# Start of a two-layer trunk kernel: all tokens loaded and transposed first, a one-block first conditioning, and two leading tiles per weight place

## The chip, the cores and the metric

The kernel runs on one core of a Trainium2 chip. The metric is the device time of one execution in microseconds (us). The engines that matter here are TensorE (PE, matrix products; it loads its stationary operand with separate instructions, PEld), VectorE (DVE), ScalarE (ACT), GpSimd (POOL) and SyncE (SP), which issues most of the DMA transfers. Each engine takes its own queue in order.

## The reference

A diffusion trunk of two layers over 128 prompt tokens and 512 sample tokens, 2048 wide. Each layer is

```python
m = silu(cond) @ ada_w[layer] + ada_b[layer]      # shift, scale, gate: 3 x 2048, one for c_ctx, one for c
h = rms_norm(x, norm_g[layer]) * (1.0 + scale) + shift
x = x + gate * (mixer(h @ w_in) @ w_out)
```

with `rms_norm` over the 2048 features of a token. Layer 0's `w_in` has 2048 rows and 6656 columns. The columns feed banded attention with a sink (query, key, value, gate) and a gated short convolution (u, b, c and a gate); layer 1 has a differential attention and a dense one. All is float32. The outputs are the new tokens and the prompt's keys and values.

Only the very start of layer 0 is touched by the change: making `h` of the 640 tokens, and the first products with `w_in`.

## The kernel before

**Layout.** Products are taken with features on the partitions: `h` is needed as 16 feature blocks (k = 0 to 15) of 128 partitions by 640 tokens, so the tokens, which lie in memory row by row, are first transposed on PE, 128 by 128 at a time. A float32 product is made of three products with split operands (`hi*hi`, `lo*hi`, `hi*lo`, lines 263 to 265): a weight tile is split on ACT (`wh`, line 227) and DVE (`wl`, line 228), and so is `h` (lines 1009 and 1010). The 640 tokens go through in two halves of 320, one for each PSUM bank (`pa`, `pb`; in the first unit the tile is called `pf`).

**Conditioning.** Shift and scale of a feature block are themselves products, of the conditioning vectors with columns of `ada_w`. `ada_on_pe` (line 173) multiplies all 16 row blocks of some columns (line 180), copies the result (line 183), transposes it back (line 186), and makes `mod` and `gsc` from it (lines 163 and 151). The loads go through four buffers of 1 MB (`ada_t`).

**Leading tiles.** While the conditioning still comes in, the kernel cannot run one output tile through all 16 feature blocks. It runs eight output tiles ("leads") side by side instead: eight *units* of two feature blocks each, and in each unit all eight leads. Two leads (`held`) keep their PSUM banks throughout. Six (`TRANS`) share the banks `pa`, `pb`: after each unit their result is added to a sum in SBUF (line 399; in the first unit it is copied, line 355). The order of the eight is sum, held, sum, held, sum, sum, sum, sum. After the first lead of a unit stands the conditioning of the next unit (`ahead`, that is `ada_group`, two column groups of 256 columns).

**Start.** Before the first unit, `first_loads` (line 975) issues the loads of scale and shift for feature blocks 0 and 1 and the first weights, transposes token blocks 0 to 2 (`x_block`, line 939: transposes at line 946, copies to `xT` at 947, sums of squares at 951), and spreads the normalisation factors over the partitions with rank-one products (`x_rows`, line 959). Token blocks 3 and 4 are loaded behind that; their transposes and squares (line 936) are put between the leads of the first unit by `between` (line 991). `first_unit` (line 331) runs the first unit by halves: tokens 0 to 319 of both feature blocks through all leads, then tokens 320 to 639.

**Weight places.** A place is a buffer of the ring `raw`, `wh`, `wl` with four each (`W_BUFS = 4`), 512 elements per partition. In the first unit a place holds two leads (`first_raws`, 2 leads x 2 blocks x 128 columns); in units 1 to 7 it holds one lead (`load_raw`, 2 blocks x 128), so half of it is unused.

**Order.** The order in which an engine takes its instructions comes from a list scheduler: the program order gives the priority, and an instruction that could start earlier is put ahead. `tc.issue_after` keeps some instructions behind a given one. Buffers are handed out by the same scheduler.

Of the kernel before, what the change touches and what calls it, by code (L numbers as in the profile page):

```python
# [20 lines left out]
P = 128  # L21
D = 2048
KT = D // P
NS = 512
# [26 lines left out]
def trunk_kernel(ctx: ExitStack, tc: tile.TileContext, I: dict, O: dict):  # L51
# [57 lines left out]
    xs = [x_load(b) for b in range(3)]  # L109
# [36 lines left out]
    def ada_done(l, cb, h=0, n=4):  # L146
        fs = slice(cb * 4 + 2 * h, cb * 4 + 2 * h + n)
        which, k0 = cb // 4, (cb % 4) * 4 + 2 * h
# [12 lines left out]
    def add_bias(l, cb, red, h=0, n=4):  # L161
        fs = slice(cb * 4 + 2 * h, cb * 4 + 2 * h + n)
        V.tensor_tensor(mod[l][:, fs, :], red, ada_b[l][:, fs][:, :, None].to_broadcast([P, n, 2]), op=ALU.add)
# [9 lines left out]
    def ada_on_pe(l, cb, h=0, n=4, ws=None):  # L173

        acc, m, wd = psT(), 16 // n, n * P
        for kt in range(KT):
            if kt % m == 0:
                w = ws[kt // m] if ws else ada_load(l, cb, kt, h, n)
# [11 lines left out]
        add_bias(l, cb, red, h, n)  # L190
        ada_done(l, cb, h, n)

    def ada_on_dve(blocks):

        for l, cb in blocks:
# [12 lines left out]
            for b in range(2):  # L208
# [11 lines left out]
                for h in range(2):  # L220
                    add_bias(l, cb + b, t[:, h, :, :, 0], h, 2)
# [103 lines left out]
    def first_raws(w_ap, cols, js):  # L325
        raw = wpool.tile([P, 2, 2, P], F32, tag="raw", name="raw")
        for i, col in enumerate(cols):
            nc.sync.dma_start(raw[:, i], w_ap[js[0] * P:js[1] * P, col:col + P].rearrange("(k p) n -> p k n", p=P))
        return raw

    def first_unit(raws, leads, trans, pps, make_h, ahead, units, between):

        pos, qd, js = units[0]
        parts = {}

        def split_two(i):
            with tc.issue_after(last_act[0].ins):
                wh, wl = split_w(raws[i])
            for j in range(2):
                parts[leads[2 * i + j]] = wh[:, j], wl[:, j]  # L340

        split_two(0)
        split_two(1)
        for half_i, sl in HV:
            for k in range(*js):
                make_h(k, half_i)
            for i, n in enumerate(leads):
                if not half_i and i in (0, 2):
                    split_two(2 + i // 2)
                if half_i and n == leads[1]:  # L350
                    ahead(*units[1][1:])
                if n in trans:
                    pp = {half_i: pproj.tile([P, 512], F32, tag="p%s0" % "ab"[i % 2], name="pf")}
                    proj_q(pp, parts[n], qd, pos, [(half_i, sl)], alone=True, js=js)
                    last_act[0] = A.copy(pps[n][half_i], pp[half_i][:, 0:HALF])
# [5 lines left out]
    def run_tiles(jobs, w_ap, make_h, fill=None, rate=0.0, ahead=None, order=(0, 1, 2, 3), before=None,  # L361
                  last=None, by_half=False, mid=False, trans=[], grace=0, cut=None, summed=None, led=None, freed=None,
                  n_lead=3, first=None, between=None):
# [13 lines left out]
        units = [(pos, qd, js) for pos, qd in enumerate(order) for js in (cut or [(0, 4)])] if leads else []  # L377
        for ui, (pos, qd, js) in enumerate(units):
            if first and ui == 0:
                first_unit(first, leads, trans, pps, make_h, ahead, units, between)  # L380
                continue
            raws = {n: load_raw(w_ap, jobs[n][0], qd, js) for n in leads[:W_BUFS]}
            parts = {n: split_w(raws[n]) for n in raws}
            for hv in [HV[:1], HV[1:]] if by_half and pos == 0 else [HV]:
                for k in range(4 * qd + js[0], 4 * qd + js[1]):
                    make_h(k, hv) if by_half else make_h(k)
                for n in leads:
                    if ahead and n == leads[1] and ui + 1 < len(units):
# [1406 lines left out]
```

## Time and profile before

| | |
|---|---|
| time, median of 3 runs | 2289.66 us (2288.84 to 2295.46) |
| profiled execution, its own time | 2289.15 us |
| its span, first to last instruction | 2287.4 us |
| PE busy | 2251.7 us, 98% |
| DVE, ACT, POOL busy | 70%, 48%, 7% |
| DMA, mean over the span | 150 GB/s; 308 GB/s in the first 70 us |

A line of a timeline gives start, length, engine, line of the kernel, operation, written tile <- read tiles, shapes and count, and in brackets how long the engine had been idle before and what ended that. A line of a group gives count, busy time, the mean of one in ns, and the idle time before. Products on PE overlap: the length of one is longer than the distance to the next.

### The profile page before, as it was taken

Reading aid. Unit: us, or ns where it says so; the run is one execution under the profiler, and the core shown is the slowest. Engines: PE = TensorE matmul, PEld = TensorE weight load, DVE = VectorE, ACT = ScalarE, POOL = GpSimd, SP = SyncE. Lnnn points to the kernel's source line nnn. Section 1 sums busy time; section 2 is a strip of 40 time slices with the busy share of each in tenths; the row PEclk is TensorE's granted clock in tenths of the full one; section 3 lists DMA queues with packets and bytes.
Section 4 is the critical chain, followed back from the end, with each engine's and each line's share of the span. In section 5 each row is a group of like instructions: output and inputs, shape, how many; then the busy total and the mean of one; then the engine's idle time right before and its main releaser. Section 6 shows DMA issues by size and latency. Waiting matters only on the chain.

```text
span 2287.4 us, 41077 instructions
## 1 busy us (share of the span) xinstructions
PE 2251.7 (98%) x15877; PEld 2175.1 (95%) x15877; DVE 1600.2 (70%) x2845; ACT 1093.0 (48%) x2317; POOL 162.3 (7%) x226
## 2 busy tenths in 40 slices
PE   7999999999999999999999999999999999999999
PEld 5889999999999999999999999999999999999999
DVE  4666969779779777787797666565666655557765
ACT  5225535244352222544474444465565676755443
POOL 1001000010000000000100001111111100000101
PEclk9999999999999999999999999999999999999999
DMA  9875545655537564865553334423223221238642
GB/s 336 265 243 195 175 151 167 184 157 170 178 118 238 178 187 144 265 179 147 170 150 114 115 113 115 142 67 100 83 64 97 71 62 51 74 103 268 182 137 62
DMA packets 381300, 344.21 MB, mean 150 GB/s; under 512 B 16418, under 2 KB 338432, under 8 KB 380592
## 3 DMA queue, kind: packets, MB, share of 16 engines
q1 hardware_dynamic: 366528, 296.66, 43.2%
q0 software_dynamic: 13856, 42.76, 5.4%
q8 instruction: 125, 2.05, 0.4%
q10 hardware_dynamic: 720, 2.16, 0.3%
q14 instruction: 71, 0.58, 0.1%
HBM read 301.93 MB, written 39.59 MB: 149 GB/s over the span
## 4 chain that ended last, share of the span: by engine, by line
PE 47%; ACT 3%; issue 2%; DVE 2%; DMA 2%; POOL 0%; SPq 0%; POOLq 0%; DVEq 0%; ACTq 0%
PE pq L585 7%; PE pq L584 7%; PE pq L583 7%; PE pb L278 2%; PE pb L277 2%; PE pa L277 2%; PE pb L279 2%; PE pa L279 2%; PE pa L278 2%; PE T L787 1%; PE T L612 1%; PE S L799 1%; PE S L801 1%; PE S L800 1%; PE pa L264 1%
## 5 line engine op out<-in xcount | busy, mean ns | idle before, releaser
L227 ACT ACTIVATE wh<-raw 128x512 fp32r<-128x512 f32 (+1 forms) x446 | 268.8, 603 | 554.7 <-PE pb L264 386.0
L228 DVE TENSOR_TENSOR wl<-raw,wh 128x512 fp32r<-128x512 f32 (+1 forms) x446 | 291.4, 654 | 208.8 <-ACT wh L227 185.8
L263 PE MATMUL pa<-h,wh 128*128 128x320 f32 x980 | 311.0, 318 | 3.6 <-ACT h L227 2.0
L264 PE MATMUL pa<-h,wh 128*128 128x320 f32 x980 | 306.1, 313 | 3.1 <-DVE h L228 2.1
L265 PE MATMUL pa<-h,wl 128*128 128x320 f32 x980 | 304.4, 311 | 0.0
L264 PE MATMUL pb<-h,wh 128*128 128x320 f32 x980 | 303.1, 309 | 0.0
L265 PE MATMUL pb<-h,wl 128*128 128x320 f32 x980 | 303.0, 309 | 0.0
L263 PE MATMUL pb<-h,wh 128*128 128x320 f32 x980 | 302.9, 310 | 0.0
L205 DVE SCALAR_TENSOR_TENSOR acc<-adaw,sT,acc 128x1024 f32<-128x1024 f32 x240 | 299.9, 1276 | 0.0
L583 PE MATMUL pq<-h,wh 128*128 128x320 f32 x672 | 208.7, 311 | 0.4 <-ACT wh L227 0.4
L585 PE MATMUL pq<-h,wl 128*128 128x320 f32 x672 | 207.9, 309 | 0.2 <-DVE wl L228 0.2
L584 PE MATMUL pq<-h,wh 128*128 128x320 f32 x672 | 207.6, 309 | 0.0
L263 PEld LDWEIGHTS pa<-h,wh 128*128 128x128 f32 x980 | 184.6, 189 | 16.5 <-issue 10.4
L264 PEld LDWEIGHTS pa<-h,wh 128*128 128x128 f32 x980 | 185.0, 189 | 10.0 <-DVE h L228 4.1
L263 PEld LDWEIGHTS pb<-h,wh 128*128 128x128 f32 x980 | 183.8, 188 | 1.8 <-issue 1.2
L265 PEld LDWEIGHTS pa<-h,wl 128*128 128x128 f32 x980 | 184.8, 189 | 0.4 <-issue 0.4
L264 PEld LDWEIGHTS pb<-h,wh 128*128 128x128 f32 x980 | 183.9, 188 | 0.2
L265 PEld LDWEIGHTS pb<-h,wl 128*128 128x128 f32 x980 | 184.0, 188 | 0.0
L585 PE MATMUL pq<-T,wl 128*128 128x320 f32 x504 | 155.1, 308 | 0.2 <-DVE wl L228 0.2
L584 PE MATMUL pq<-T,wh 128*128 128x320 f32 x504 | 155.3, 308 | 0.0
L583 PE MATMUL pq<-T,wh 128*128 128x320 f32 x504 | 155.0, 308 | 0.1
L277 PE MATMUL pa<-h,wh 128*128 128x320 f32 x448 | 146.1, 326 | 0.0
(452 smaller groups left out, 5399.9 us busy)
## 6 DMA issues: line engine op xcount, KB each, us to landing
adaw<-in_ada_w SPq DMA_DIRECT2D x128, 512.0 KB, 4.2
raw<-in_ev_w_in SPq DMA_DIRECT2D x176, 256.0 KB, 3.5
raw<-in_od_w_in SPq DMA_DIRECT2D x154, 256.0 KB, 2.9
ada<-in_ada_w SPq DMA_DIRECT2D x32, 1024.0 KB, 7.6
w<-in_od_w_in SPq DMA_DIRECT2D x27, 512.0 KB, 3.9
yd<-y POOLq DMA_DIRECT2D x32, 320.0 KB, 3.4
yin<-yd SPq DMA_DIRECT2D x32, 320.0 KB, 4.3
w<-yd SPq DMA_DIRECT2D x32, 320.0 KB, 3.9
```

The source lines that it names most:

```text
L205: V.scalar_tensor_tensor(out=acc[c], in0=w, scalar=sT[:, kt, c:c + 1], in1=acc[c], op0=ALU.mult, op1=ALU.add)
L227: A.activation(hi, x, AF.Copy)
L228: V.tensor_sub(lo, x, hi)
L263: PE.matmul(ps, wh[:, i, :], hi[:, sl], start=(j == js[0] if alone else (pos == 0 and j == 0)), stop=False)
L264: PE.matmul(ps, wh[:, i, :], lo[:, sl], start=False, stop=False)
L265: last_mm[0] = PE.matmul(ps, wl[:, i, :], hi[:, sl], start=False, stop=(j == js[1] - 1 if alone else (pos == 3 and j == 3)))
L277: PE.matmul(ps, wh[:, j, :], hi[:, sl], start=(qd == 0 and j == 0), stop=False)
L278: PE.matmul(ps, wh[:, j, :], lo[:, sl], start=False, stop=False)
L279: PE.matmul(ps, wl[:, j, :], hi[:, sl], start=False, stop=(qd == 3 and j == 3))
L583: PE.matmul(ps, wh[:, j, :], hi, start=(new and h == 0 and j == 0), stop=False, **kw)
L584: PE.matmul(ps, wh[:, j, :], lo, start=False, stop=False, **kw)
L585: PE.matmul(ps, wl[:, j, :], hi, start=False, stop=(h == 1 and j == 3), **kw)
```

## The change

All five token blocks are loaded at the very start, ahead of conditioning and weights, and `first_loads` transposes all five before the first unit; `between` and the separate squares of blocks 3 and 4 are gone. Conditioning is addressed by feature block (`b0`) instead of by halves of four. The first conditioning covers feature block 0 alone (128 columns of scale, 128 of shift, one load of 1 MB each); that of block 1 stands after the first lead of the first unit. The first unit is run block by block, over all 640 tokens: block 0 through all leads, with results of the summed leads copied, then block 1 with results added. In all eight units a weight place holds two leads. The weights of the next unit are loaded during a unit, at leads 2, 3, 5 and 6, and the splits are made up to two places ahead.

```diff
-    xs = [x_load(b) for b in range(3)]
+    xs = [x_load(b) for b in range(5)]
...
-    def ada_load(l, cb, kt, h, n):
+    def ada_load(l, cb, kt, b0, n):
         m = 16 // n
         w = ada_t[0].rearrange("p (k n) -> p k n", k=m)
         ada_t.append(ada_t.pop(0))
-        nc.sync.dma_start(w, I["ada_w"][l, kt * P:(kt + m) * P, cb * 512 + h * 256:cb * 512 + h * 256 + n * P]
+        nc.sync.dma_start(w, I["ada_w"][l, kt * P:(kt + m) * P, cb * 512 + b0 * P:cb * 512 + (b0 + n) * P]
                           .rearrange("(k p) n -> p k n", p=P))
...
-    def first_unit(raws, leads, trans, pps, make_h, ahead, units, between):
...
-        split_two(0)
-        split_two(1)
-        for half_i, sl in HV:
-            for k in range(*js):
-                make_h(k, half_i)
-            for i, n in enumerate(leads):
-                if not half_i and i in (0, 2):
-                    split_two(2 + i // 2)
-                if half_i and n == leads[1]:
-                    ahead(*units[1][1:])
-                if n in trans:
-                    pp = {half_i: pproj.tile([P, 512], F32, tag="p%s0" % "ab"[i % 2], name="pf")}
-                    proj_q(pp, parts[n], qd, pos, [(half_i, sl)], alone=True, js=js)
-                    last_act[0] = A.copy(pps[n][half_i], pp[half_i][:, 0:HALF])
-                else:
-                    proj_q(pps[n], parts[n], qd, pos, [(half_i, sl)], js=js)
-                if not half_i:
-                    between(i)
+    def lead_units(raws, w_ap, jobs, leads, sums, pps, make_h, ahead, units, summed):
+
+        two = len(leads) // 2
+        cols = [(jobs[leads[2 * p]][0], jobs[leads[2 * p + 1]][0]) for p in range(two)]
+        parts = []
+
+        def split_to(q):
+            while len(parts) < 2 * min(q + 1, two * len(units)):
+                p = len(parts) // 2
+                with tc.issue_after(last_act[0].ins) if p < two else ExitStack():
+                    wh, wl = split_w(raws[p])
+                parts.extend((wh[:, j], wl[:, j]) for j in range(2))
+
+        def one_block(u, k, n, part, pp):
+            alone = n in sums
+            wh, wl = part
+            hi, lo = hs[k]
+            j = k % 2
+            for h, sl in HV:
+                ps = pp[h][:, 0:HALF]
+                PE.matmul(ps, wh[:, j, :], hi[:, sl], start=(alone or k == 0), stop=False)
+                PE.matmul(ps, wh[:, j, :], lo[:, sl], start=False, stop=False)
+                last_mm[0] = PE.matmul(ps, wl[:, j, :], hi[:, sl], start=False, stop=alone)
+
+        for ui, (pos, qd, js) in enumerate(units):
+            k0 = 4 * qd + js[0]
+            split_to(ui * two)
+            for c in range(2 if ui == 0 else 1):
+                ks = [c] if ui == 0 else [k0, k0 + 1]
+                for k in ks:
+                    make_h(k)
+                for i, n in enumerate(leads):
+                    if i == 1 and ui == 0 and c == 0:
+                        ahead(0, (1, 2))
+                    elif i == 1 and ui + 1 < len(units):
+                        ahead(*units[ui + 1][1:])
+                    if ui or not c:
+                        split_to(ui * two + min(i // 2 + 1, two - (ui == 0)))
+                    elif i == len(leads) - 2:
+                        split_to(two)
+                    if (ui or c) and i in (2, 3, 5, 6) and ui + 1 < len(units):
+                        _, q, j = units[ui + 1]
+                        raws.append(load_two(w_ap, cols[(2, 3, 5, 6).index(i)], 4 * q + j[0]))
+                    part = parts[2 * ui * two + i]
+                    pp = new_pp(0) if n in sums else pps[n]
+                    if ui == 0:
+                        one_block(ui, c, n, part, pp)
+                    else:
+                        proj_q(pp, part, qd, pos, alone=n in sums, js=js)
+                    if n in sums:
+                        for h, sl in HV:
+                            if ui == 0 and c == 0:
+                                last_act[0] = A.copy(sums[n][:, sl], pp[h][:, 0:HALF])
+                            else:
+                                V.tensor_add(sums[n][:, sl], sums[n][:, sl], pp[h][:, 0:HALF])
+                        summed(ui, n, pps[n])
...
     def first_loads(cols):
 
-        scale = [ada_load(0, 4, kt, 0, 2) for kt in (0, 8)]
-        raws = [first_raws(I["ev_w_in"][0], cols[i:i + 2], (0, 2)) for i in (0, 2)]
-        shift = [ada_load(0, 0, kt, 0, 2) for kt in (0, 8)]
-        raws += [first_raws(I["ev_w_in"][0], cols[i:i + 2], (0, 2)) for i in (4, 6)]
-        xs.extend(x_load(b) for b in (3, 4))
+        scale = [ada_load(0, 4, 0, 0, 1)]
+        raws = [load_two(I["ev_w_in"][0], cols[0:2], 0)]
+        shift = [ada_load(0, 0, 0, 0, 1)]
+        raws += [load_two(I["ev_w_in"][0], cols[i:i + 2], 0) for i in (2, 4, 6)]
         x_block(0, xs[0])
         vec_rows(0, 80, rows_a, 32)
-        x_block(1, xs[1])
-        x_block(2, xs[2])
-        ada_on_pe(0, 4, 0, 2, scale)
-        x_rows((0, 1, 2))
-        ada_on_pe(0, 0, 0, 2, shift)
+        for b in range(1, 5):
+            x_block(b, xs[b])
+        last_act[0] = put[0]
+        ada_on_pe(0, 4, 0, 1, scale)
+        x_rows((0, 1, 2, 3))
+        x_rows((4,))
+        vec_rows(80, 77, rows_b, 0)
+        ada_on_pe(0, 0, 0, 1, shift)
         return raws
```

More of the change, by code (lines that the diff above doesn't have):

```diff
@@ L377, in run_tiles @@
         units = [(pos, qd, js) for pos, qd in enumerate(order) for js in (cut or [(0, 4)])] if leads else []
+        if first:
+            lead_units(first, w_ap, jobs, leads, sums, pps, make_h, ahead, units, summed)
+            units = []
         for ui, (pos, qd, js) in enumerate(units):
[L379 to L382, printed above, removed]
+            raws = {n: load_raw(w_ap, jobs[n][0], qd, js) for n in leads}
             parts = {n: split_w(raws[n]) for n in raws}
@@ L1149, in trunk_kernel @@
     run_tiles(jobs, I["ev_w_in"][0], h0_maker, fill0, FILL0, ada_group, trans=TRANS, grace=GRACE, cut=((0, 2), (2, 4)),
-              summed=keep, led=even_start, freed=ada_start, first=raws, between=between)
+              summed=keep, led=even_start, freed=ada_start, first=raws)
     drain(prep)
```

94 lines of the change are left out of this document (27 added, 67 removed).

## The prediction

> **What bounds the kernel now.** I read the page first, then the busy time by stage, then the start of the kernel in order of time on TensorE (PE), VectorE (DVE) and ScalarE (ACT). The page, whose span is 2287.4 us:
>
> ```profile
> PE 2251.7 (98%) x15877; PEld 2175.1 (95%) x15877; DVE 1600.2 (70%) x2845; ACT 1093.0 (48%) x2317; POOL 162.3 (7%) x226
> ...
> PE   7999999999999999999999999999999999999999
> ```
>
> PE is busy for 98% of the span, and of the 40 slices only the first lacks its 9. I cut the span there: up to the first weight product (30.05), the first unit of the eight leading tiles (to 56.70), units 1 to 7 (to 187.60), and the rest, which the change does not touch:
>
> ```profile
> 0.00:30.05 30.05, 16.01 (x124) 9.90 (x124) 11.22 (x30) 12.73 (x24) 6.06 (x15) 0.94 0.98 337
> 30.05:56.70 26.65, 26.22 (x201) 21.86 (x202) 15.38 (x38) 17.66 (x46) 1.10 (x2) 0.94 1.03 336
> 56.70:187.60 130.90, 129.40 (x1082) 112.40 (x1080) 88.12 (x222) 38.69 (x94) 1.24 (x3) 1.00 0.78 249
> 187.60:2287.40 2099.80, 2080.10 (x14473) 2030.97 (x14472) 1485.46 (x2555) 1023.91 (x2155) 153.88 (x207) 1.00 0.46 139
> ```
>
> Columns: PE, weight loads, DVE, ACT, POOL, clock, DMA share, GB/s. The lead-in is bound by DMA (share 0.98, 337 GB/s, PE busy 16 of 30 us). From 30 us on PE is the bound. So the change is worth what it takes off PE after 30 us, plus what it does to the instant of the first product; what it moves into the lead-in is free as long as DMA still ends last there.
>
> The end of the lead-in:
>
> ```profile
> 25.99 1.82 PE L180 MATMUL T<-ada,sT 128*32 128x256 f32 x16 [1.78 <-DMA ada<-in_ada_w]
> 28.34 0.69 PE L186 MATMUL T<-ident,ada_sb 128*128 128x128 f32 x2 [0.53 <-ACT ada_sb L183]
> 30.09 0.64 PE L263 MATMUL pf<-h,wh 128*128 128x320 f32 x1 [1.06 <-ACT h L1009]
> ...
> 32.92 0.35 PE L263 MATMUL pa<-h,wh 128*128 128x320 f32 x1
> ```
>
> The second half of the shift weights lands at 25.99; products, two transposes and h follow, 4.1 us in all, and then the first product. The first 11 products take 2.83 us.
>
> **The lead-in, part by part.** What must land before the first product, by these issue rows:
>
> ```profile
> ada<-in_ada_w SPq DMA_DIRECT2D x13, 1024.0 KB, 9.1
> raw<-in_ev_w_in SPq DMA_DIRECT2D x20, 128.0 KB, 5.8
> xb<-in_x_sample ACTq DMA_DIRECT2D x4, 512.0 KB, 6.5
> ```
>
> Before: three token blocks (6 x 512 KB), four conditioning loads (4 x 1024 KB) and two weight places (4 x 128 KB), 7.9 MB. After: five token blocks (10 x 512 KB), two conditioning loads, one weight place, 7.6 MB. SP now issues blocks 3 and 4 ahead of all this, and the second weight place no longer stands ahead of the shift load; POOL's queue only gets two powers earlier. The 0.26 MB less are 0.75 us at 348 GB/s. Against it, the one-block conditioning is read in runs of 512 bytes where the two-block one has runs of 1024. DMA at work on the long runs, and in a stretch that is mostly 512-byte weights:
>
> ```profile
> 50.00:52.00 2.00, 2.00 (x24) 1.22 (x23) 1.33 (x4) 0.46 (x2) 0.00 (x0) 1.00 1.09 348
> 58.00:60.00 2.00, 2.00 (x33) 1.29 (x36) 0.78 (x2) 0.00 (x0) 0.00 (x0) 1.00 1.06 316
> ```
>
> 2.1 MB at 316 instead of 348 GB/s cost 0.6 us. So the shift lands 0.15 us earlier, at 25.8. [...]
>
> Can five blocks be through by then? Per block ACT does two squares and one copy; the transposes of blocks 3 and 4 and their rank-one rows now stand on PE after 30 us:
>
> ```profile
> 8.16 1.00 ACT L951 ACTIVATE sqj<-xb 128x1024 f32<-128x1024 f32 x1
> ...
> 29.47 1.02 ACT L1009 ACTIVATE h<-ht,mod 128x320 fp32r<-128x320 f32 x2 [1.18 <-DVE mod L163]
> ```
> ```profile
> 34.35 1.03 PE L946 MATMUL T<-ident,xb 128*128 128x128 f32 x8
> 35.15 0.39 PE L264 MATMUL Sp<-h,wh 128*128 128x320 f32 x1
> ...
> 42.61 0.38 PE L963 MATMUL T<-ident,rx 128*128 128x128 f32 x2
> ...
> 43.80 1.91 PE L180 MATMUL T<-ada,sT 128*32 128x256 f32 x26
> ```
> ```profile
> L951 ACT ACTIVATE sqj<-xb 128x1024 f32<-128x1024 f32 x6 | 6.1, 1024 | 1.1 <-DMA xb<-in_x_sample 1.0
> L951 ACT ACTIVATION_READ_ACCUMULATOR sqj<-xb 128x1 f32 x6 | 1.1, 187 | 0.0
> L947 ACT COPY xT<-T 128x512 f32<-128x512 f32 x5 | 2.9, 574 | 2.2 <-PE T L946 2.2
> ```
>
> ACT: 2 x (1.02 + 0.19) + 0.57 = 3.0 us a block, so from 8.2 us (its first square) five blocks end at 23.2. The rank-one rows take PE 1.2 us (42.61 to 43.80) and, with the power before and the copy behind, about 2 by my estimate. That is 25.2, just ahead of the shift. If this cover fails, each us late is a us on the path.
>
> After the landing all 16 row blocks of the shift are multiplied (32 products of 128 columns), where before only the last 8 were left (16 of 256, 1.82 us at the low clock). The trace has no such product: half the time of the quoted row's for each gives 1.8 us, the same time for each 3.6. I take 1.9, near the first, since the columns are halved. h is then made for 512 tokens at once instead of 320; at 0.5 us each (1.02 for two) that is 0.3 more in proportion, of which the earlier landing gives 0.15 back. First product: 30.1 + 0.1 + 0.15, which I leave at 30.1. Bounds: 27.5, when the clock is full and rows wait for nothing, and 32.
>
> The clock was granted thus:
>
> ```profile
> 12.00:26.00 14.00, 10.13 (x94) 6.18 (x93) 8.24 (x19) 6.85 (x13) 1.40 (x3) 1.00 1.10 358
> ...
> 22.70:26.10 3.40, 1.22 (x21) 0.61 (x24) 1.02 (x2) 0.48 (x1) 0.00 (x0) 1.00 1.12 351
> 26.10:32.90 6.80, 5.21 (x28) 3.58 (x28) 2.00 (x5) 1.91 (x5) 0.00 (x0) 0.50 1.04 404
> ```
>
> A thin stretch (1.22 of 3.40 us) is followed by half the clock until 32.9. After the change PE is thin again between block 4 (23.2) and the shift, so I keep the loss as it is. [...]
>
> **The first unit.** One tile's step in the steady part (12 products), DVE's sums with the work between them, and the conditioning within the first unit:
>
> ```profile
> 92.88 0.34 PE L263 MATMUL pa<-h,wh 128*128 128x320 f32 x1
> ...
> 94.67 0.34 PE L263 MATMUL pa<-h,wh 128*128 128x320 f32 x1
> ```
> ```profile
> 93.07 0.49 DVE L399 TENSOR_TENSOR sum<-sum,pb 128x320 f32<-128x320 f32 x1 [0.40 <-PE pb L265]
> 93.48 0.42 DVE L228 TENSOR_TENSOR wl<-raw,wh 128x256 fp32r<-128x256 f32 x1
> 93.98 0.49 DVE L399 TENSOR_TENSOR sum<-sum,pa 128x320 f32<-128x320 f32 x1
> 94.86 0.49 DVE L399 TENSOR_TENSOR sum<-sum,pb 128x320 f32<-128x320 f32 x1 [0.39 <-PE pb L265]
> ```
> ```profile
> L180 PE MATMUL T<-ada,sT 128*32 128x256 f32 x64 | 4.7, 385 | 0.0
> L186 PE MATMUL T<-ident,ada_sb 128*128 128x128 f32 x4 | 0.9, 273 | 0.0
> ```
>
> A tile's 12 products take 1.79 us, 0.149 each; the unit's 96 are 14.3. Its 26.65 us: 14.3, plus 1.2 for the low clock (2.83 - 11 x 0.149), plus the next unit's conditioning 4.7 + 0.5 (half of the transposes' 0.9 overlaps), plus 32 token transposes at 0.80 per 8 = 3.2, plus the rank-one rows 1.2 (42.61 to 43.80). That is 25.1; 1.5 is waiting.
>
> Removed: 3.2 + 1.2 = 4.4 us, now under DMA's wait in the lead-in. Added: the conditioning of block 1, two calls of 32 products of 128 columns, where the unit's 64 products of 256 columns and four transposes are 5.2 us: between 2.6 us (time goes with columns) and 5.0 (only the transposes halve). I take 3.0, near the first, as the columns halve but the weight loads do not. Added too: the unit runs block by block, so a tile that is summed elsewhere has only 3 products (0.44 us) per bank before the bank must be emptied. A bank's turn is then 0.44 + 0.19 (pipeline tail: 0.34 - 0.149) + the copy or sum + about 0.1 of waiting:
>
> ```profile
> L355 ACT COPY sum<-pf 128x320 f32<-128x320 f32 x12 | 5.0, 424 | 3.7 <-PE pf L265 3.7
> ```
>
> That is 1.15 us with the copy (block 0) and 1.22 with the 0.49 us sum (block 1), against 0.88 of products: up to 0.3 us at each of 8 turns where two such tiles follow one another, 2.4 in all. They cost nothing if PE has the 3.0 + 5.2 us of conditioning to put there, and 5 if DVE is crowded as well: in block 1 it has 12 sums (5.8) and the two next h's, four pieces each of this row and its like:
>
> ```profile
> L1010 DVE SCALAR_TENSOR_TENSOR h<-ht,mod,h 128x128 fp32r<-128x128 f32 (+1 forms) x25 | 12.6, 538 | 3.5 <-ACT h L1009 3.4
> ```
>
> That is 8 x 0.54 = 4.3, together 10.1 and the small work beside PE's 7.1 + 5.2. I take 2.3 for the turns, near the 2.4, and this replaces the 1.5 of waiting. New unit: 14.3 + 1.2 + 3.0 + 5.2 + 2.3 = 26.0, so it ends at 56.1 instead of 56.7: **-0.6**. DMA stays ahead: up to unit 1's conditioning 14.7 MB must land (5.2 tokens, 4.2 + 4.2 conditioning, 1.0 weights), at the first two stages' 337 GB/s by 43.6, and PE wants it near 50.
>
> **Units 1 to 7.** Same products, same loads. Two things change. One wait goes: a tile's split waited for a place in the old ring, and a sum stood behind it on DVE.
>
> ```profile
> 151.56 0.43 DVE L228 TENSOR_TENSOR wl<-raw,wh 128x256 fp32r<-128x256 f32 x1 [1.78 <-ACT wh L227]
> 152.53 0.38 PE L263 MATMUL pa<-h,wh 128*128 128x320 f32 x1 [1.49 <-DVE sum L399]
> ```
>
> Four shared places hold all eight tiles, so I drop it: -1.5. In its place the shared split is 0.69 us (measured in the first unit) against 0.42:
>
> ```profile
> L228 DVE TENSOR_TENSOR wl<-raw,wh 128x512 fp32r<-128x512 f32 x4 | 2.7, 690 | 3.4 <-ACT wh L227 3.4
> ```
>
> Between a pb sum and the next pa sum the quoted rows leave just the 0.42 us that a split takes: the pa sum ends at 94.47 and PE uses the bank again at 94.67. So a shared split there delays PE by 0.69 - 0.42 = 0.27. Four splits in seven units could make 7.6; if most go where the two tiles that are summed in place give room, it is one in two units: 1.0. Sum: **-0.5**, bounds -1.5 and +6. After 187.6 nothing changes. Total -1.1 on the profiled execution's 2289.15 (its span and 1.75 around it): 2288.05, that is 2288 (the median, 2289.66, lies 0.5 above that execution).
>
> **The rivals.** *All gaps fill (faster).* The first product comes at 27.5, clock full, turns filled by conditioning: the unit is 14.3 + 2.6 + 5.2 = 22.1 and ends at 49.6, -7.1; with -1.5 later, 2280.6. For it: DMA is ahead of PE in every unit, and the 1.22 us busy before 26.1 shows room. Against: ACT's 23.2 and the low clock.
>
> *The shared split takes the place of the wait (slower).* Its place is DVE between two sums of consecutive tiles; it decides once a split there exceeds 0.42 us, and 0.69 does. All 28 of them: 2289.15 - 0.6 + 7.6 = 2296. For it: the four rows of sums show no slack. Against: a split may start as soon as its place is free, up to a unit ahead.
>
> *PE waits for conditioning (the gain goes unseen).* PE takes its queue in order; unit 2's conditioning ends 19.9 MB into the stream, at 337 GB/s 59.1 us, and PE may reach it one tile into unit 1, at 57.9: +1.2, and as much again for its second half. Once only, for after that DMA (5.2 MB, 15.6 us a unit) outruns PE's 18.7. 2290.5.
>
> **How the numbers follow.** What this kernel's measurement can tell from no change is about 0.3%, 6.9 us. Forecast 0.37, PE waiting for conditioning 0.05: both within it, 0.42. All gaps fill: 0.34, faster. Shared split: 0.24, slower. The forecast's own range is 2283 to 2293. The range over all reaches to 2279 (gaps filled, and the late waits gone with them) and to 2298 (all shared splits late, and 2 us of the first unit's bound of 5 for its turns).
>
> **What would show it.** Right: first weight product within 1 us of 30.1; no L946 after it; unit 0 ending at 55 to 57; PE's idle in units 1 to 7 under 2 us. Wrong: a first product before 28 or after 32; PE waiting for a sum or copy for over 4 us in the first unit; rows "PE pa <- DVE sum" repeated in each unit; a different busy time after the lead stage.

## The result, and the profile after

| | kernel before | kernel changed |
|---|---|---|
| median, in the measurement of the change | 2293.63 us | 2287.91 us (20 runs) |
| ratio, 95% interval | 1 | 0.9978 [0.9971, 0.9985] |
| ratio when measured again, twice | 1 | 0.9974 [0.9966, 0.9982] and 0.9978 [0.9968, 0.9987] |
| profiled execution, its own time | 2289.15 us | 2292.61 us |

The change saves 5 to 6 us, 0.2%. That is inside the 0.3% named in the prediction, yet three measurements agree on it to 0.04%. The two profiled executions on their own say the opposite (+3.5 us): the changed kernel's was the slowest of its 20, and that of the kernel before was one of its quickest. So the stages are read below from a second pair as well, whose traces were taken side by side.

First the page of the changed kernel and its busy time by stage (cut at the first weight product, at the end of the first unit, and at the end of the eighth). The columns of the stages are length, PE, weight loads, DVE, ACT, POOL, clock, DMA share, GB/s, as before.

```profile
PE 2257.0 (99%) x15941; PEld 2178.5 (95%) x15941; DVE 1603.5 (70%) x2830; ACT 1087.0 (47%) x2281; POOL 162.6 (7%) x226
```

```profile
0.00:32.70 32.70, 21.03 (x191) 15.40 (x191) 15.42 (x40) 17.97 (x34) 7.17 (x17) 1.00 1.01 318
32.70:58.70 26.00, 24.96 (x219) 18.89 (x222) 16.09 (x40) 12.37 (x30) 0.00 (x0) 1.00 1.04 327
58.70:186.60 127.90, 127.90 (x1064) 110.82 (x1065) 85.72 (x196) 33.29 (x65) 1.67 (x3) 1.00 0.83 258
186.60:2290.80 2104.20, 2083.11 (x14472) 2033.43 (x14471) 1486.30 (x2555) 1023.35 (x2155) 153.75 (x206) 1.00 0.46 139
```

The lead-in grew from 30.05 to 32.70 us. The first unit takes 26.00, units 1 to 7 take 127.90 without any idle PE, and the first two stages show the clock at 1.00 where they showed 0.94.

The second pair, same columns, is cut at the first weight product, at the end of unit 1, at the end of unit 7, and at the first transposes behind the lead stage. The kernel before:

```profile
0.00:28.97 28.97, 16.49 (x124) 11.09 (x124) 11.24 (x31) 12.80 (x24) 6.05 (x15) 1.00 0.98 335
28.97:75.30 46.33, 45.94 (x371) 37.31 (x372) 28.45 (x71) 23.72 (x62) 1.10 (x2) 1.00 0.94 302
75.30:187.60 112.30, 110.38 (x913) 97.29 (x913) 75.14 (x190) 32.83 (x79) 1.48 (x3) 0.98 0.79 249
187.60:211.10 23.50, 22.39 (x152) 21.85 (x152) 13.05 (x32) 9.06 (x27) 2.51 (x4) 1.00 0.70 247
211.10:2289.90 2078.80, 2058.71 (x14320) 2010.11 (x14320) 1472.88 (x2524) 1013.50 (x2128) 151.01 (x203) 1.00 0.46 138
```

And the changed one:

```profile
0.00:32.70 32.70, 20.96 (x191) 15.47 (x191) 15.33 (x40) 18.02 (x34) 7.15 (x17) 1.00 1.01 319
32.70:76.50 43.80, 43.30 (x367) 34.31 (x368) 29.21 (x71) 17.59 (x40) 0.00 (x0) 1.00 1.06 333
76.50:186.10 109.60, 109.60 (x914) 95.40 (x913) 72.65 (x165) 28.04 (x55) 1.67 (x3) 1.00 0.79 246
186.10:208.80 22.70, 22.06 (x152) 21.78 (x151) 12.96 (x32) 9.03 (x27) 2.33 (x3) 1.00 0.69 249
208.80:2287.30 2078.50, 2058.50 (x14320) 2010.30 (x14320) 1473.15 (x2524) 1013.99 (x2128) 151.05 (x203) 1.00 0.46 138
```

From top to bottom: +3.7 in the lead-in, -2.5 up to the end of unit 1, -2.7 in units 2 to 7, -0.8 behind them, -0.3 in the rest. So at the start the change only moves work: unit 1 ends at 76.5 instead of 75.3. What it gains, it gains later. The third row of the kernel before includes a stretch at half the clock; in another trace of it, which shows 1.00 where this one has the half clock, units 2 to 7 take 111.7 and the stretch behind them 24.3: in sum 136.0, against 135.8 here.

The end of the lead-in on PE (profiled execution of the changed kernel):

```profile
24.81 1.09 PE L951 MATMUL T<-ident,xb 128*128 128x128 f32 x7
26.08 1.08 PE L180 MATMUL T<-ada,sT 128*32 128x128 f32 x32 [0.18 <-DVE xT L952]
27.55 0.33 PE L186 MATMUL T<-ident,ada_sb 128*128 128x128 f32 x1 [0.39 <-ACT ada_sb L183]
27.71 1.29 PE L966 MATMUL T<-ident,rx 128*128 128x128 f32 x10
29.45 0.29 PE L131 MATMUL T<-ident,rows_b 77*128 77x77 f32 x1 [0.45 <-ACT tables L967]
29.67 1.08 PE L180 MATMUL T<-ada,sT 128*32 128x128 f32 x32
31.19 0.33 PE L186 MATMUL T<-ident,ada_sb 128*128 128x128 f32 x1 [0.44 <-ACT ada_sb L183]
31.45 1.08 PE L180 MATMUL T<-ada,sT 128*32 128x128 f32 x32
32.73 0.56 PE L351 MATMUL pa<-h,wh 128*128 128x320 f32 x2 [0.20 <-ACT h L1004]
```

None of these rows waits for DMA. Scale, normalisation rows, powers and shift stand in one chain on PE behind the last transposes, with waits for ACT's copies between them. In the second trace the last row of conditioning waits 0.56 us for a load, with the first product at 32.74 all the same. So the lead-in is no longer bound by its loads, as the prediction had it, but by this chain.

### The profile page after: what moved, and what is told of

It reads as the page before. It is cut to its first block, busy times and chain, and to the rows that moved or that the text cites. A ratio compares the mean times of both kernels' runs of the same rounds, so it can differ in the third digit from the quotient of the medians.

```text
span 2290.8 us, 41085 instructions
## 1 busy us (share of the span) xinstructions
PE 2257.0 (99%) x15941; PEld 2178.5 (95%) x15941; DVE 1603.5 (70%) x2830; ACT 1087.0 (47%) x2281; POOL 162.6 (7%) x226
## 3 DMA queue, kind: packets, MB, share of 16 engines
q8 instruction: 125, 2.05, 0.4%
## 4 chain that ended last, share of the span: by engine, by line
PE 87%; DVE 5%; ACT 4%; DMA 3%; issue 2%; POOL 0%; SPq 0%; DVEq 0%; POOLq 0%; ACTq 0%
PE pq L597 7%; PE pq L596 7%; PE pq L595 7%; PE pa L263 6%; PE pa L264 6%; PE pa L265 6%; PE pb L264 6%; PE pb L263 5%; PE pb L265 5%; PE pb L278 2%; PE pb L277 2%; PE pa L277 2%; PE pb L279 2%; PE pa L279 2%; PE pa L278 2%; PE T L799 2%
## 5 line engine op out<-in xcount | busy, mean ns | idle before, releaser
L227 ACT ACTIVATE wh<-raw 128x512 fp32r<-128x512 f32 x418 | 263.3, 630 | 553.9 <-PE pb L264 388.0
L228 DVE TENSOR_TENSOR wl<-raw,wh 128x512 fp32r<-128x512 f32 x418 | 287.8, 689 | 200.4 <-ACT wh L227 176.8
```

The source lines that it names most:

```text
L227: A.activation(hi, x, AF.Copy)
L228: V.tensor_sub(lo, x, hi)
```

## The experiments

The measure within a trace is the start of the key transposes, some 280 us behind the lead stage: 468.5 in three traces of the kernel before, 466.1 to 466.6 in three of the changed one. Each such instant is of one execution.

**The two kernels again.**

> The changed kernel once more, for a second profile beside the first. In the first profile the first weight product comes at 32.7 us (before the change 30.1), and the key transposes that follow the lead stage at 466.6 (before 468.5). Theory A, the gain is made within the lead stage: the first product again within 1 us of 32.7, the key transposes at 465 to 468, and the time about 5 us below the kernel before. Rival B, the gain comes from later stages, by another order of the same work: then the two profiles agree to 1 us up to 468 us, and what sets the times apart lies behind.

> The changed kernel once more, to be compared on one chip with the two below. Theory (two parts: about 2 us of lead stage, shown by the key transposes at 466.3 to 466.6 instead of 468.5; and the granted clock, whose mean over an execution is .998 or .999 in all executions of the changed kernel and .995 to .999 in those of the kernel before): 2286.5 to 2288.5 us, ratio about 0.9975, mean clock .998 to .999 again. Rival (the clock goes with the chip or the hour, not with the kernel): in one of the batches the kernel before has the high clock as well, and the ratio is then 0.9985 to 0.999.

> The kernel before once more, for a second profile. In the first profile half the clock was granted from 26.2 to 33.0 us, the first weight product came at 30.1 us and the key transposes at 468.5 us, and that execution (2289.15 us) was 4 us faster than the median of the later runs. If the time before varies with the clock in the lead-in: the stretch of half clock begins or ends elsewhere, and the key transposes move with it by 1 to 4 us. Rival: the lead stage repeats to 0.5 us (key transposes at 468 to 469), and the variation lies behind.

> The kernel before once more with a profile. The two profiles so far, of executions with mean clocks of .998, lose the clock once in the first 130 us for 6.8 us or not at all. Theory: an execution of low mean clock (.995 or .996) shows further stretches at half the clock in the first 130 us, 6.8 us each a row of 3.4 us of lost work. Rival: its lost clock lies after the lead stage, in 187 to 2288 us, where the change touches nothing.

The changed kernel: 2286.68 and 2287.93 us, key transposes at 466.25 and 466.14. The kernel before, single executions: 2290.67 and 2291.67 us, key transposes at 468.50 and 468.53. So the lead stage repeats and gives 2.2 us, as Theory A of again_after said; the ratios say 5 to 6. What sets apart executions of one kernel lies behind it, in these traces: the three of the kernel before agree to 0.04 us at the key transposes, and their spans differ by 2.5 us (2287.38, 2288.90 and 2289.90). The first trace of the changed kernel ends 5.8 us after its second; 4.0 of them arise between 2092 and 2138 us, a stretch of 3.4 us at half the clock among them. The runs list the mean granted clock of each execution, and over all 91 executions of the kernel before that ran beside the experiments, and all 43 of the changed kernel, it sorts the times:

| mean granted clock | before: executions, mean us | changed: executions, mean us |
|---|---|---|
| 0.994 and 0.995 | 13, 2296.8 | none |
| 0.996 | 16, 2294.4 | none |
| 0.997 | 36, 2291.5 | none |
| 0.998 | 19, 2291.2 | 26, 2288.7 |
| 0.999 | 7, 2289.3 | 17, 2286.5 |

At equal clock the changed kernel is 2.5 to 2.8 us ahead, near the 2.2 of the traces. It also never has the low clocks: its mean is 0.9984, the other's 0.9969. A straight line through the 91 gives 1.84 us for each 0.001, so these 0.0015 would be worth 2.8 us, if the clock is what costs the time; the line alone doesn't show that. My rival, that the clock goes with the chip and not with the kernel, fell: 0.9969 in each of the three batches.

Where the kernel before loses the clock: in its first profile, behind the thin stretch that the prediction quotes; in the second, nowhere in the lead stage; in the third, here (timeline of PE, then two stretches):

```profile
148.57 0.31 PE L265 MATMUL pb<-h,wl 128*128 128x320 f32 x1
150.80 0.48 PE L263 MATMUL pa<-h,wh 128*128 128x320 f32 x1 [1.91 <-DVE sum L399]
```

```profile
147.50:150.90 3.40, 1.49 (x11) 1.25 (x10) 1.20 (x4) 0.73 (x2) 0.00 (x0) 1.00 1.06 349
150.90:154.30 3.40, 3.40 (x14) 3.40 (x15) 1.03 (x4) 0.32 (x1) 0.00 (x0) 0.51 0.64 190
```

PE waits 1.91 us for a sum, was busy for 1.49 of the 3.40 us around that wait, and works the next 3.40 us at half the clock. The second profile of the kernel before has the same wait, and keeps its clock:

```profile
150.77 0.39 PE L263 MATMUL pa<-h,wh 128*128 128x320 f32 x1 [1.94 <-DVE sum L399]
```

```profile
146.80:150.20 3.40, 2.03 (x14) 1.76 (x12) 0.89 (x3) 0.73 (x2) 0.00 (x0) 1.00 1.12 363
150.20:153.60 3.40, 2.83 (x19) 2.84 (x20) 2.44 (x7) 0.42 (x1) 0.00 (x0) 1.00 0.85 253
```

Stretches at half the clock last 3.4 or 6.8 us in the profiles of the two kernels (first trace of the kernel before: 26.1 to 32.9 and 1132.0 to 1135.4; first trace of the changed kernel: 1130.2 to 1137.0 and 2133.7 to 2137.1), and 13.6 us in e4 below. In the 3.40 us ahead of such a stretch PE was busy for 1.22 us (first trace, at 22.7), 1.49 (third), and 0.08, 0.99 and 1.26 (e2, e8 and e4 below). In the second trace the two stretches quoted have 2.03 and 2.83 us of busy PE; but the 3.40 us from 148.8 have 1.46, as few as in the third, and show 1.00 as well. So the same wait of 2 us is followed by half the clock in one execution and not in the next. What decides between them is not shown.

What such a loss costs in the end is another question. From the first product up to the wait the third trace runs level with the second, to 0.1 us; from 153 to 184 us the same products start 1.5 us later (worked out from their starts). In the first trace, with its loss in the lead-in, they start 2.2 us later from 31 to 150. Then the delays vanish:

| trace of the kernel before | at half the clock in the lead stage | transposes behind unit 7 | key transposes |
|---|---|---|---|
| first | 6.8 us | 211.11 | 468.54 |
| second | none | 211.34 | 468.50 |
| third | 3.4 us | 211.13 | 468.53 |

The second trace, which comes to these places earlier, waits there (PE's timeline), where the other two don't:

```profile
184.89 0.39 PE L263 MATMUL pa<-h,wh 128*128 128x320 f32 x1 [0.77 <-DVE sum L399]
200.82 0.87 PE L612 MATMUL T<-ident,stg 128*128 128x128 f32 x5 [1.00 <-ACT stg L605]
```

That is what the rival of again_before said: the lead stage ends at the same instant whatever the clock did in it. So the 2.8 us are not found in any trace: the losses that were caught, worth 1.5 and 2.2 us where they happen, are taken up by later waits. An execution of the kernel before at 0.995 was not caught in a profile. That it loses the clock more often than later waits can take up would fit the table, in which 0.997 is no slower than 0.998 by more than 0.3 us while 0.996 and less are 3 to 6 us slower; it is not shown. Nor is the rival of third_before refuted, that the slow executions lose their time behind the lead stage.

**e8: the kernel before, with products that nobody reads in two waits of the lead-in.** `warm(n, after)` issues n products of the identity with itself behind the instruction named, once between the two halves of the shift, once behind its transposes.

```diff
+            if ws and cb == 0 and kt == 8:
+                warm(6, last_ada[-1])
...
         ada_on_pe(0, 0, 0, 2, shift)
+        warm(8, last_tr[0])
```

> The kernel before with 14 products that nobody reads (identity by identity, 0.118 us each at the full clock) put into waits that PE has in any case: 6 where it waits for the second half of the shift weights, 8 where it waits for the first h. They fill about 0.7 of 1.0 to 1.8 us and 0.9 of 1.3 us. Theory (the kernel before loses the granted clock for some us in a part of its executions because PE is idle in the lead-in, and that is half of what the change gives): first product within 0.3 us of 28.9 to 30.1, key transposes at 468 to 469, mean clock .998 to .999 in nearly all executions, time 2 to 3 us less than the kernel before, ratio about 0.999. Rival (the clock is lost later or by chance, and the products in the lead-in have no bearing on it): mean clock .995 to .999 as before, ratio 1.000.

2291.14 us, ratio 0.9993 [0.9984, 1.0002]; mean clock 0.9983, all 11 executions at 0.998 or 0.999, where the kernel before had 0.9969 in the same batch. Key transposes at 468.85. So with these products in the lead-in the mean clock is higher, by 0.0014; that is shown. The gain in time has the expected size in the means (2290.78 against 2293.62), but its interval reaches past 1, so it is not shown. Each added product takes two rows on PE: they filled 1.60 and 1.95 us, twice what was expected. Its own trace is 2.5 us ahead of the kernel before at the transposes behind unit 7 (208.58), and loses this lead in a wait of 2.40 us for ACT at 236.9, behind which it also runs 3.4 us at half the clock (PE was busy 0.99 of the 3.40 us from 234.3).

**e6: the same with 24 such products, put less carefully.**

```diff
+        warm(12)
         ada_on_pe(0, 0, 0, 2, shift)
+        with tc.issue_after(last_tr[0].ins):
+            warm(12)
```

> The kernel before with 24 products more that no one reads, 12 ahead of the shift products and 12 behind them, where PE waits. If the low clock costs the kernel before (11 products at half speed, 1.2 us, and the shift products 0.7): full clock at the first product, time 1 to 3 us below the kernel before. Rival (the clock is not what sets the first unit; its waits only move): time within 0.5 us of the kernel before, or above it by the 2 us that the added products take.

2291.40 us, ratio 0.9998 [0.9988, 1.0008], mean clock 0.9984. The clock came, but the first product stands at 32.25 and the key transposes at 473.20, 4.7 us later: the added products stood in the path. The two parts together, 4.7 us lost and 2.7 gained by the line, would make it 2 us slower; the mean is 0.9 faster than the kernel before's in that batch, and the trace is of an execution 2 us above the median. So here the sum of the two parts doesn't come out.

**e1: the changed kernel with the old first conditioning of two blocks.** Block 1 then has no conditioning of its own behind the first product.

```diff
-        scale = [ada_load(0, 4, 0, 0, 1)]
+        scale = [ada_load(0, 4, kt, 0, 2) for kt in (0, 8)]
...
-        shift = [ada_load(0, 0, 0, 0, 1)]
+        shift = [ada_load(0, 0, kt, 0, 2) for kt in (0, 8)]
```

> The first conditioning is again of two feature blocks (two loads of 1 MB each for scale and shift); all else as in the changed kernel. Theory A (the lead-in ends when the token chain and then DMA end): 2.1 MB more ahead of the first product are 6 us at 340 GB/s, the shift lands near 31 instead of 25.3, and the first product comes at 35 to 36; PE saves the 2.2 us of the second block's conditioning behind it; time +1 to +2 us against the changed kernel. Rival C (the one-block conditioning is what pays): first product the same, time +4 us or more.

2290.70 us, ratio 0.9995 [0.9985, 1.0005], apart from the changed kernel's 0.9974 [0.9966, 0.9982] in that batch. The timeline of PE:

```profile
31.52 1.07 PE L180 MATMUL T<-ada,sT 128*32 128x256 f32 x16 [0.86 <-DMA ada<-in_ada_w]
...
34.79 0.41 PE L351 MATMUL pa<-h,wh 128*128 128x320 f32 x1 [1.22 <-ACT h L1002]
```

With five token blocks ahead of it, the 2 MB shift lands last again, the first product comes 2.05 us later and the key transposes at 468.52. Without the one-block conditioning nothing of the 2.2 us is left in the trace. The medians differ by 4.0, as Rival C said, though the first product moved as Theory A said; the other 1.8 are not located. The mean clock is 0.9983, as high as the changed kernel's, and the key transposes are those of the kernel before: by the line this run should be 2.6 us faster than the kernel before, and it is 1.1 in the means.

**e2: the kernel before with all tokens loaded and transposed first, nothing else.**

```diff
-    xs = [x_load(b) for b in range(3)]
+    xs = [x_load(b) for b in range(5)]
...
-        x_block(1, xs[1])
-        x_block(2, xs[2])
+        for b in range(1, 5):
+            x_block(b, xs[b])
```

> The kernel before with one part of the change alone: all five token blocks loaded first, and transposed ahead of the products; conditioning of two blocks, first unit by halves, single places as before. If the lead-in ends when DMA ends: 2.1 MB more ahead of the first product, which comes at 35 to 36 us; PE saves 4.4 us behind it and 1.2 us of low clock; time within 1 us of the kernel before. Rival (the moved transposes are the whole gain): time 4 us or more below the kernel before.

2293.15 us, ratio 1.0006 [0.9996, 1.0017]: alone this part gains nothing, as expected; the medians differ by 1.7 us, and the interval holds 1. First product 34.29, key transposes 469.02. The wait for a sum is at its longest here, 3.38 us, and is followed by the half clock:

```profile
128.50:131.90 3.40, 0.08 (x1) 0.12 (x2) 1.05 (x3) 0.77 (x2) 0.00 (x0) 1.00 1.11 368
131.90:135.30 3.40, 3.40 (x13) 3.40 (x14) 0.99 (x3) 0.23 (x1) 0.00 (x0) 0.50 0.58 174
```

**e3: the changed kernel with one lead per weight place in units 1 to 7, as before.**

```diff
-        for ui, (pos, qd, js) in enumerate(units):
+        for ui, (pos, qd, js) in enumerate(units[:1]):
...
+                    if n not in parts:
+                        parts[n] = split_w(load_raw(w_ap, jobs[n][0], qd, js))
```

> Units 1 to 7 take weights in single places again (one tile of 128x256 per place), loaded and split as before the change; the first unit and the lead-in as in the changed kernel. If the gain is the PE work moved out of the lead stage: the first product at 32.7, the time within 1 us of the changed kernel's. Rival D (the shared places bring the gain, by taking waits out of units 1 to 7): the wait of PE for DVE's sum comes back (1.5 us or more in the profile), and the time is 2 to 4 us above the changed kernel's.

2288.56 us, ratio 0.9985 [0.9975, 0.9994]; the intervals overlap with the changed kernel's, so the 1.9 us between the medians are not settled. The trace shows both sides of the part. The wait for a sum is back:

```profile
150.81 0.39 PE L263 MATMUL pa<-h,wh 128*128 128x320 f32 x1 [0.82 <-DVE sum L419]
```

and the others of units 2 to 6 take 18.7 to 18.8 us, where with shared places four of these five take 19.1 to 19.2 (one 18.6). In the changed kernel that is read here (DVE, then PE):

```profile
130.14 0.49 DVE L385 TENSOR_TENSOR sum<-sum,pb 128x320 f32<-128x320 f32 x1 [0.39 <-PE pb L265]
130.65 0.69 DVE L228 TENSOR_TENSOR wl<-raw,wh 128x512 fp32r<-128x512 f32 x1
131.26 0.48 DVE L385 TENSOR_TENSOR sum<-sum,pa 128x320 f32<-128x320 f32 x1
```

```profile
131.55 0.31 PE L265 MATMUL pb<-h,wl 128*128 128x320 f32 x1
131.80 0.42 PE L263 MATMUL pa<-h,wh 128*128 128x320 f32 x1
```

The shared split of 0.69 us holds the sum back, and the next product comes 0.25 behind the last one instead of 0.15. Over units 2 to 5 the step from a pb product to a pa product is 0.187 us in the mean (20 steps, eight of them 0.23 to 0.25), 0.04 over the usual 0.147: 0.2 us a unit, of the 0.3 to 0.4 by which most of these units are longer.

**e7: the shared split in two pieces.**

```diff
-                    wh, wl = split_w(raws[p])
+                    for j in range(2):
+                        split(wh[:, j], wl[:, j], raws[p][:, j])
```

> The changed kernel with the splits of a shared weight place in units 1 to 7 cut into two of 256 columns. Theory A (a shared split of 0.69 us on DVE between a pb sum and the next pa sum delays PE by about 0.27, once in a unit): a piece is 0.42 us again, units 1 to 6 take 18.8 instead of 19.1, the key transposes come at 464.5 instead of 466.3, and the time is 1.5 to 2 us less than the changed kernel's in this batch, about 2285. Rival B (the 0.3 us of a unit come from the conditioning's place or from the order, and DVE's extra instructions cost as much as they free): units stay at 19.1 and the time is within 0.7 us of the changed kernel's. Rival C (the wait of a sum behind a split that has no free place, 1.5 us once, comes back as the scheduler spreads the halves): one unit is a us longer.

2293.64 us, ratio 0.9998 [0.9987, 1.0008], beside 0.9978 for the changed kernel in that batch: 5.7 us slower, which neither theory nor rival said. The step from pb to pa is 0.147 us again, so what Theory A wanted removed is gone. But the scheduler laid the conditioning differently. PE's timeline in unit 3, the changed kernel first:

```profile
97.32 1.93 PE L180 MATMUL T<-ada,sT 128*32 128x256 f32 x32
99.19 0.41 PE L263 MATMUL pa<-h,wh 128*128 128x320 f32 x1
...
100.19 1.93 PE L180 MATMUL T<-ada,sT 128*32 128x256 f32 x32
```

```profile
100.55 1.07 PE L180 MATMUL T<-ada,sT 128*32 128x256 f32 x16
101.55 0.41 PE L265 MATMUL pa<-h,wl 128*128 128x320 f32 x1
101.89 1.07 PE L180 MATMUL T<-ada,sT 128*32 128x256 f32 x16
102.90 0.41 PE L263 MATMUL pb<-h,wh 128*128 128x320 f32 x1
```

In e7 the second 32 products come in two pieces with a weight product between. Going from weight products to conditioning takes 0.239 us from start to start, going back 0.309, where two weight products are 0.149 apart: 0.25 us lost with each piece. Units 2 to 5 of e7 have 16 such returns where the changed kernel has 9. That is 0.4 of the 0.95 us that a unit lost (from last sum to last sum); the rest is not told apart. The key transposes come at 469.36, 3.2 us later; the other 2.5 of the 5.7 us are not located.

**e5: the changed kernel, with most of the fifth token block behind the shift.**

```diff
+        with tc.issue_after(last_ada[0].ins):
+            for g in range(1, 4):
+                x_group(4, xs[4], g)
+            vec_rows(80, 77, rows_b, 0)
```

> The changed kernel with another order on PE in the lead-in: of the last token block only the first group of transposes stands ahead of scale, rows and shift; the other three groups, and the small vectors, come behind the shift products. All work is kept. If PE's order in the lead-in sets the first product (shift landed at 25.3, its products at 29.7): shift products at 25.5 to 27, first weight product at 29 to 30.5, PE still busy so that the clock stays full; time 2 to 3 us below the changed kernel. Rival (the clock falls to half as in the wide ring, since PE has less to do ahead): first product at 30 to 32 and the time equal to or above the changed kernel's.

First product at 29.59, 3.1 us earlier, as expected, and the mean clock is 0.9985 over its 11 executions; but the 2 to 3 us that this should gain do not come. 2289.63 us, ratio 0.9986 [0.9977, 0.9995], no better than the changed kernel's ratios, and key transposes at 467.84, 1.2 to 1.7 us later than the changed kernel's. The first unit ends at 58.3, against 58.2 to 58.7. The moved work stands on PE on either side of the first product, and behind it a load ends later than PE:

```profile
35.63 1.08 PE L182 MATMUL T<-ada,sT 128*32 128x128 f32 x32 [0.87 <-DMA ada<-in_ada_w]
```

That is the conditioning of block 1, which in the changed kernel is awaited as well (0.71 us at 35.00 in its second trace). The first product's date, on which the prediction spent most of its working, is not what the time hangs on.

**e4: the changed kernel, token transposes through four banks instead of two.**

```diff
-            ta = psT()
+            tag = ("pa0", "pb0", "pa1", "pb1")[g]
+            ta = pproj.tile([P, 512], F32, tag=tag, name="xt")
```

> The token transposes go through the four idle product banks instead of the ring of two; all else as in the changed kernel. If the ring of two is what makes the token stage take 0.72 us per group of four transposes (26.0 us at its end): the groups follow at 0.55 to 0.65, the stage ends at 23 to 24, the first product comes 2 to 3 us earlier, at 30 to 31, and the time is 2 to 3 us lower than the changed kernel's. Rival E (DMA holds the lead-in: the shift lands at 25.3 and its chain follows): the stage ends earlier but the first product stays within 0.5 us of 32.7.

2294.65 us, ratio 1.0012 [1.0003, 1.0022]. The trace is of an execution 3.9 us above this median. The last transpose starts at 20.71, 5 us earlier, so the ring of two banks was what paced them. Then PE waits for the normalisation:

```profile
29.55 0.79 PE L967 MATMUL T<-ident,rx 128*128 128x128 f32 x2 [2.79 <-POOL rx L961]
```

```profile
23.00:26.40 3.40, 1.26 (x9) 1.07 (x9) 1.57 (x7) 3.40 (x7) 1.10 (x2) 1.00 0.96 260
26.40:40.00 13.60, 8.99 (x77) 5.42 (x76) 3.82 (x11) 5.32 (x13) 0.55 (x1) 0.50 0.98 276
```

ACT is busy without a pause up to 26.4 (squares), the clock is at half for 13.6 us, the first product comes at 34.70 and the key transposes at 474.45. Both expectations missed it: PE was done sooner, then waited, and ran slower afterwards.

## Why the prediction was right in its number, and where not

The forecast of 2288 was met (2287.91), and that is luck: it was formed as -1.1 on an execution of 2289.15, which lies 4.5 us below the median of the kernel before (2293.63), and the gain was 5 to 6 us instead of 1.1. The two errors cancel. The case of the likeliest outcome, a difference within 0.3%, came true. Of its steps:

- **First product at 30.1, DMA last.** Wrong: 32.7, past the 32 that the text itself gave as the sign of an error. The step that failed is "ACT: 3.0 us a block, from 8.2 us five blocks end at 23.2". ACT's work was right and not the pace. Blocks 1 to 4 start on PE at 13.6, behind block 0 and the first powers, and go through two banks, four transposes in 0.72 us; the last copy ends at 26.6. e4 shows that the banks set this. Then the chain on PE follows, which the text had hidden under the shift's landing.
- **The removed 4.4 us, "now under DMA's wait".** Wrong for the same reason: 3.7 later at the first product, 2.5 won back by the end of unit 1 in the second pair.
- **One-block conditioning, 3.0 us for two calls, bounds 2.6 and 5.0.** Too high: 32 products of 128 columns take 1.08 us, two calls 2.2, and one of them fits into the wait ahead of the first product.
- **Turns of a bank, 2.3 us, and a first unit of 26.0.** The unit's length is right (26.0 here, 25.5 in the second pair) by terms that offset each other. The 1.2 of low clock did not come, the turns show no wait for copies, and one of the two calls above stands ahead of the unit. In their place the stretch of the second pair holds 13 products of unit 2's conditioning, 8 weight products of unit 1, and nine pieces of conditioning between the leads, each paid, by estimate, with the 0.25 us of the change-over found in e7.
- **The clock, "I keep the loss as it is".** Wrong: the clock was 1.00 from 17.5 us, amid the transposes, to the end of the lead stage at 186.6, and the wait of 1.91 us that was followed by half the clock in the third trace of the kernel before is gone. By the line through the executions this is the largest miss, 2.8 us; no trace shows where it enters the time. The prediction's own row, 14 us of mostly transposes at 1.00 (6.1 of the 10.1 us of busy PE), pointed that way, and the conclusion was not drawn from it. In the changed kernel:

```profile
17.50:26.00 8.50, 7.46 (x48) 4.96 (x48) 6.72 (x14) 6.08 (x12) 1.65 (x3) 1.00 1.16 314
```

  PE does nothing but transposes in these 8.50 us, at the full clock.
- **Units 1 to 7: wait dropped, -1.5; shared splits, +1.0.** Right in both mechanisms. The wait is gone in three traces, and was 1.9 rather than 1.5 us in the kernel before's two later ones. The splits cost 0.2 to 0.3 us a unit, nearer 1.5 in all. From the end of unit 1 to that of unit 7: 109.6 in three traces, against 110.3, 111.7 and 112.3.
- **"After 187.6 nothing changes."** Not quite: 22.7 to 22.8 us to the next transposes instead of 23.3 to 24.4. In the longest of these, the second trace of the kernel before, PE waits 1.00 us for ACT's copy at 200.8 (shown above), which the changed kernel doesn't; the rest is open.
- **Rivals.** "All gaps fill" was wrong about the first product (27.5) and right that the clock would be full. "PE waits for conditioning" shows in the first trace, 1.0 us at 56.6, for the DMA of `ada`. It is absent in the two later traces. "The shared split takes the place of the wait" has its mechanism, but not at all 28 splits.

## What to carry to other kernels

Ask of every wait on TensorE not only how long it is but what clock the trace shows behind it: here a wait of 1.91 us was followed by 3.4 us at half the clock in one execution, and one of 1.94 us was not in another. Then follow the delay on: here later waits took up 1.5 and 2.2 us of it, and a correlation of time and clock says more than the traces bear out. Work that is moved ahead of the first product isn't free because DMA ends last there (the first product came at 32.7 instead of 30.05 us); follow the order on the moved-to engine to the end, for it may become the chain itself. And when two profiles disagree with the medians, look at the mean clock of all executions before explaining the profiles.

## What the runs showed of the hardware

- The spread of the kernel before (2287 to 2301 us) goes with the granted clock: 1.84 us for each 0.001 over 91 executions, correlation -0.74. Where the slowest executions lose it is in no trace.
- Delays of 1.5 and 2.2 us from half the clock in the lead stage were gone at 211 us: 211.11, 211.34 and 211.13 with 6.8, 0 and 3.4 us at half the clock before.
- Stretches at half the clock were 3.4, 6.8 and 13.6 us long. A wait of 1.91 us was followed by one (third trace of the kernel before), a wait of 1.94 us was not (second trace). Further on, 3.40 us with 1.93 us of busy PE (first trace of the kernel before, from 1128.6) and with 2.52 (first trace of the changed kernel, from 1126.8) were followed by half the clock, and 3.40 us with 1.46 (second trace of the kernel before, from 148.8) were not: the busy time of a stretch alone doesn't tell.
- Changing between weight products and conditioning products on PE costs 0.25 us for going and returning together, worked out from the starts in units 2 to 5.
